# Sums of weight quarters by accumulating DMAs in a one-level Strassen-Winograd MLP product

## The chip, the cores and the metric

The kernel runs on one core of a Trainium2 chip. The metric is the device time of one execution in microseconds (us). Its engines have queues of their own: TensorE (PE; its weight loads are listed as PEld), VectorE (DVE), ScalarE (ACT), GpSimd (POOL) and SyncE (SP), which here only issues DMAs.

## What is computed

One layer of a decoder trunk for 512 tokens of width 1024, all in float32: a norm, an input projection, a pooling mixer and a sparse attention mixer that are merged by gates, and an MLP. The change touches the first product of the MLP:

```
h = rms_norm(x, norm_mlp[l])
x = x + jnp.square(jax.nn.relu(h @ w_ff1[l])) @ w_ff2[l]
return rms_norm(x, norm_final)
```

`w_ff1` is 1024 x 4096 and `w_ff2` 4096 x 1024.

## The kernel before

Every float32 matrix is used as a high part (rounded to float32r by ScalarE's copy) and a low part (the rest, a subtraction on VectorE), and every product is three matmuls: high x high, high x low, low x high.

**The stages.** Input projection, attention and mixers come first. Then the output projection `wo` is applied (`tm3` and `tm3_resident`, line 1226), the residual is normed and turned by `to_fm` (lines 1189 to 1217), and four chunks of the MLP follow, c = 0 to 3 (lines 1320 to 1376). A chunk makes 1024 hidden columns in two groups of 512 (the first MLP product), and then multiplies them by 1024 rows of `w_ff2` (the second, keys `f2...`, eight weight blocks).

**A group.** A group is the product of a 1024 x 512 piece of `w_ff1` with the turned activations, done as one level of Strassen-Winograd with seven products in place of eight. The piece is cut into four quarters of 512 x 256: "21" is columns half 2, rows half 1, and so on. Seven weight operands are made: A11, A12, A22 are quarters, and S1 = 21 + 22, S2 = S1 - 11, S3 = 11 - 21, S4 = 12 - S2. The activations have T1 to T4 likewise (`XB`, `XT`, lines 1211 to 1216), each split into high and low once. `product` (1235) runs 24 matmuls on 256 tokens for one operand. The class `Group` (1248) combines the results: `s` is a copy of the A11 result, `u2 = S2 result + s`, `u3 = S3 result + u2`, and so on; `NEEDS` says that A22 comes after `u3` and S4 after the last sum. `act` (1307) takes relu, square and the split of the result.

**The order of products.** Chunk 0 uses `FIRST` (line 136): A11 and A12 of both groups, then S1, S3, S2 of each group, then A22, S4 of each, since T1 to T4 are finished late there. Chunks 1 to 3 run group 0 and then group 1 in the order `IN_TURN` (line 137): A11, S2, S3, S1, A12, A22, S4.

**Loading and preparing weights.** `LD` is the list of loads in order and `WL` the list of weight operands in order of use. A load (`emit_load`, 167) goes to the SP queue into one of eight 512 KB buffers: four called `raw` and, in this part of the kernel, four pieces of `oT`. When an operand has been made from a buffer, `give_back` (197) lends it to the next load. `group_steps` (216) prepares an operand of a group: ScalarE's copy to the high part (line 226), VectorE's subtraction for the low part (228), and, in four places, the sums of quarters on VectorE: line 231 makes S1 in a spare piece of `GB`, 233 makes S3, 235 makes S2, 238 makes S4. Prepared operands lie in three slots (`w`, twice, and `w3`). `ahead` (294) is called between matmuls and prepares at most the two operands behind the one in use, since a slot is free only when the product three places back is done. Other weight blocks are prepared in halves by `emit_prep_half` (lines 277 and 279; in the earlier stage the second half's low part is on GpSimd).

**What sets the order on the engines.** The program gives an order of instructions, with generators in `side` stepped between matmuls (`step_side`). A scheduler then places each instruction in its engine's queue by its own estimate of when its inputs are ready, so an instruction can stand earlier or later than written. Each queue runs in order, and an instruction that waits holds up those behind it.

Of the kernel before, what the change touches and what calls it, by code (L numbers as in the profile page):

```python
# [62 lines left out]
def trunk(ctx: ExitStack, tc: tile.TileContext, A, out):  # L63
# [70 lines left out]
            add_rows(f"wo{h}{i}", w_o, 256 * i, 512 * h)  # L134
    GROUPS = {}
    FIRST = ("A11", "A12"), ("S1", "S3", "S2"), ("A22", "S4")
    IN_TURN = ("A11", "S2", "S3", "S1", "A12", "A22", "S4")

    def add_group(c, g):

        c0 = 1024 * c + 512 * g
        GROUPS[c, g] = {"raw": {}, "at": {}}
        for q in ("11", "21", "22", "12"):
            r0, o = 512 * (int(q[1]) - 1), c0 + 256 * (int(q[0]) - 1)
            GROUPS[c, g]["at"][q] = len(LD)
            LD.append(([(w_f1[r0:r0 + 512, o:o + 256].rearrange("(k p) c -> p k c", p=128), 0)], (c, g, q)))

    for c in range(4):
        for g in range(2):
# [42 lines left out]

    def strassen_on():

        return st["load"] >= GROUPS[0, 0]["at"]["11"]

    def give_back(*tiles):
        spare.extend(tiles)
# [6 lines left out]
    def slot_of(i):  # L205
# [7 lines left out]
            return slots_hl[-1]  # L213
        return [wp.tile([128, 1024], FR, tag=f"w{e}", bufs=2, name=f"w{e}{i}") for e in "hl"]

    def group_steps(i):

        c, g, o = WL[i][1]
        G = GROUPS[c, g]
        while len(G["raw"]) < 4:  # L220
            assert emit_load()
        r = G["raw"]
        sm = GBf[:, 1024 + 1024 * g:2048 + 1024 * g]
        src = {"A11": r["11"], "A12": r["12"], "A22": r["22"], "S1": sm, "S2": r["11"], "S3": r["21"], "S4": r["12"]}[o]
        h, l = slot_of(i)
        ACT.activation(h, src, AF.Copy)
        yield
        DVE.tensor_tensor(l, src, h.bitcast(F32), op=ALU.subtract)
        if o == "A11":
            yield  # L230
            DVE.tensor_tensor(sm, r["21"], r["22"], op=ALU.add)
            yield
            DVE.tensor_tensor(r["21"], r["11"], r["21"], op=ALU.subtract)
            yield
            DVE.tensor_tensor(r["11"], sm, r["11"], op=ALU.subtract)
        elif o == "A12":
            yield
            DVE.tensor_tensor(r["12"], r["12"], r["11"], op=ALU.subtract)
        G["done"] = G.get("done", "") + o
        dead = {"S3": "21", "A22": "22", "S4": "12"}.get(o)  # L240
        if o in ("A12", "S2") and "A12" in G["done"] and "S2" in G["done"]:
            dead = "11"
        hls[i] = tuple(x.rearrange("p (a b) -> p a b", a=4) for x in (h, l))
        if dead:
            give_back(r[dead])

    def emit_prep_half():

        i = st["prep"]
        if i >= len(WL):  # L250
            return
        if not isinstance(WL[i][1], int):
            if "gen" not in part:
                part["gen"] = group_steps(i)
            if next(part["gen"], True):
                part.clear()
                st["prep"] += 1
            return
        at = WL[i][1]
        if "h" not in part:  # L260
            while st["load"] <= at:
                assert emit_load()
            if WL[i][0] in dest:
                h, l = dest[WL[i][0]][:2]
            else:
                h, l = slot_of(i)
            part.update(h=h, l=l, half=0)
        h, l = part["h"], part["l"]
        t, a, b = raws[at]
        n = a * b  # L270
        cut = (a // 2) * b
        sl = slice(0, cut) if part["half"] == 0 else slice(cut, n)
        if sl.stop > sl.start:
            if mode["first"]:
                POOL.tensor_scalar(h[:, sl], t[:, sl], 1.0, 1.0, op0=ALU.mult, op1=ALU.mult)
            else:
                ACT.activation(h[:, sl], t[:, sl], AF.Copy)  # L277
            eng = POOL if mode["first"] or part["half"] and mode["pool"] else DVE
            eng.tensor_tensor(l[:, sl], t[:, sl], h[:, sl].bitcast(F32), op=ALU.subtract)  # L279
        if part["half"] == 0:  # L280
            part["half"] = 1
            return
        part.clear()
        st["prep"] += 1
        raws.pop(at)
        if st["load"] > RAW + GROUPS[0, 0]["at"]["11"]:
            give_back(t)
        else:
            emit_load()
            if st["kept"] == RAW:  # L290
                give_back()
        hls[i] = (h[:, :n].rearrange("p (a b) -> p a b", a=a), l[:, :n].rearrange("p (a b) -> p a b", a=a))
# [873 lines left out]
    with ExitStack() as c3:  # L1166
        q3 = c3.enter_context(pool("q3"))
        mT = (q3.tile([128, 8, S], FR, name="mH"), q3.tile([128, 8, S], FR, name="mL"))
        W1 = (q3.tile([128, 8, S], FR, name="W1H"), q3.tile([128, 8, S], FR, name="W1L"))
        keep([f"wo1{i}" for i in range(4)], W1)  # L1170
        ACT.activation(tick, GB[:, 7, 0:1], AF.Sqrt)

        def split_m(j):
            ACT.activation(mT[0][:, j, :], GB[:, j, :], AF.Copy)
            DVE.tensor_tensor(mT[1][:, j, :], GB[:, j, :], mT[0][:, j, :].bitcast(F32), op=ALU.subtract)
        split_m(0)
        split_m(1)
        for j in range(2, 8):
            def post(ps, j=j):
                merge(j, ps)  # L1180
                split_m(j)
            fm3(f"pn{j}", post, OT)

        def post0(t, ps):
            add_x(t, 0, ps)
            square_sum(t, 0)
        tm3("wo", 0, mT, post0)

        def to_fm(t):
            xs = q3.tile([128, D], F32, tag="xs", bufs=1, name="xs")  # L1190
            add_x(t, 1, PS1[t])
            square_sum(t, 1)
            normed(t, xs)
            for _ in range(5):
                yield
            th, sl = t // 2, slice(128 * (t % 2), 128 * (t % 2) + 128)
            for a in range(2):
                pt = bank()
                for k in range(4):
                    PE.transpose(pt[:, 128 * k:128 * k + 128], xs[:, 512 * a + 128 * k:512 * a + 128 * k + 128], ident)  # L1200
                src = pt[:, :].rearrange("p (k c) -> p k c", k=4)
                b = f"{a + 1}{th + 1}"
                if b != "12":
                    ACT.activation(XB[b][0][:, :, sl], src, AF.Copy)
                ACT.activation(XQ[b][:, :, sl], src, AF.Copy)
                if b != "12":
                    DVE.tensor_tensor(XB[b][1][:, :, sl], src, XB[b][0][:, :, sl].bitcast(F32), op=ALU.subtract)
                yield
            if th == 0:
                return  # L1210
            for o, d, x, y in (("T1", XT, XQ["12"], XQ["11"]), ("T3", XQ["12"], XQ["22"], XQ["12"]),
                               ("T2", XQ["11"], XQ["22"], XT), ("T4", XQ["21"], XQ["21"], XQ["11"])):
                DVE.tensor_tensor(d[:, :, sl], x[:, :, sl], y[:, :, sl], op=ALU.subtract)
                ACT.activation(XB[o][0][:, :, sl], d[:, :, sl], AF.Copy)  # L1214
                yield
                DVE.tensor_tensor(XB[o][1][:, :, sl], d[:, :, sl], XB[o][0][:, :, sl].bitcast(F32), op=ALU.subtract)
            turned[0] += t == 3

        PS1 = {}

        def post1(t, ps):
            PS1[t] = ps
            g = to_fm(t)
            next(g)
            side.append(g)
        tm3_resident("wo", 1, mT, post1)
# [21 lines left out]
    class Group:  # L1248


        def __init__(self, c, g, aT):
            self.c, self.g, self.aT = c, g, aT
            self.s = pair(GBf, 6 + g)
            self.u2, self.u3, self.c21 = pair(MAf, 6 + g), pair(MAf, g), pair(MAf, 2 + g)
            self.ps, self.done = {}, set()
# [21 lines left out]
        def main(self):  # L1277
# [4 lines left out]
            while "S2" not in self.done:  # L1282
                yield
            yield
            DVE.tensor_tensor(self.u2, self.ps["b"], self.s, op=ALU.add)
            while "S3" not in self.done:
                yield
            yield
# [18 lines left out]
        def act(self, src, f, th):  # L1307
            yield
            r = p4.tile([128, 512], F32, tag="r", bufs=2, name="r")
            ACT.activation(r, src, AF.Relu)  # L1310
            ACT.activation(r, r, AF.Square)
            hi, lo = (x[:, 4 * self.g + 2 * f:4 * self.g + 2 * f + 2, 256 * th:256 * th + 256] for x in self.aT)
            r = r.rearrange("p (f t) -> p f t", f=2)
            ACT.activation(hi, r, AF.Copy)
            yield
            yield
            DVE.tensor_tensor(lo, r, hi.bitcast(F32), op=ALU.subtract)
# [77 lines left out]
```

## Time and profile before

| | |
|---|---|
| median of 3 runs | 828.61 us (827.01 to 829.36) |
| the profiled execution | 829.27 us, its span 827.5 us |
| PE busy | 801.9 us (97%) |
| DVE, ACT, POOL busy | 569.8, 459.8, 166.2 us |
| mean granted clock of TensorE | 0.994 |
| read from HBM | 72.81 MB, 91 GB/s over the span |

A row of the order of time (timeline) gives the start in us, the duration in us, the engine, the line, the operation, the tiles (output <- inputs), shapes and a count of merged instructions, and in brackets how long the engine was idle before it and what ended that. A row of a table by line ends with busy time and mean ns of one, then the idle time before it with what released it. A row of waits reads "who waited, for whom: us in total, times, longest". A row of DMA issues ends with KB each and the median us from issue to landing. Busy time of matmuls is modelled, and their bars overlap.

### The profile page before, as it was taken

The numbers are of one execution on the slowest core, as the hardware profiler recorded it, in microseconds if no ns is written. First come the engines' busy times: TensorE is split into PE (matmuls) and PEld (weight loads), VectorE is DVE, ScalarE is ACT, GpSimd is POOL, SyncE is SP. The second block draws the span as 40 slices with busy tenths as digits, with TensorE's granted clock in tenths as the row PEclk, the third lists the DMA queues.
The fourth block names the chain that finished last, engine by engine and source line by source line (L and its number), as shares of the span: only waits on it lengthen the run. The fifth ranks groups of instructions, "written<-read, shape, count | busy, mean of one in ns | idle before, by whom it ended". The sixth has DMA issues, their size and how long they took to land.

```text
span 827.5 us, 12810 instructions
## 1 busy us (share of the span) xinstructions
PE 801.9 (97%) x4649; PEld 695.0 (84%) x4649; DVE 569.8 (69%) x1155; ACT 459.8 (56%) x945; POOL 166.2 (20%) x235
## 2 busy tenths in 40 slices
PE   7999999999998999999999989999999999999997
PEld 4889878887887888888787879889988899889986
DVE  7797744537978888887674788646864586458813
ACT  6566443337868888898333584622761376227711
POOL 6000000027765756652223000000000000000000
PEclk9999999999999999999999999999999999999999
DMA  9363632331030101115425004431353035313202
GB/s 304 96 178 114 183 90 89 103 96 44 14 90 27 40 26 40 47 58 178 153 77 178 1 26 162 147 99 30 116 161 100 28 102 159 97 51 103 78 0 103
DMA packets 83289, 78.36 MB, mean 95 GB/s; under 512 B 3573, under 2 KB 69657, under 8 KB 83226
## 3 DMA queue, kind: packets, MB, share of 16 engines
q1 hardware_dynamic: 82938, 76.75, 30.2%
q8 instruction: 37, 0.61, 0.3%
q10 hardware_dynamic: 288, 0.79, 0.3%
q14 instruction: 26, 0.21, 0.1%
HBM read 72.81 MB, written 2.10 MB: 91 GB/s over the span
## 4 chain that ended last, share of the span: by engine, by line
PE 80%; DVE 8%; ACT 4%; POOL 2%; issue 2%; DMA 2%; SPq 0%; POOLq 0%; ACTq 0%; DVEq 0%
PE psB L320 27%; PE psF L320 20%; PE psB L1241 18%; PE psO L1003 3%; PE psT L969 3%; PE psS L908 2%; PE psV L320 2%; DVE P L930 2%; DVE PT L984 1%; DMA raw<-w_out 1%; PE psF L374 1%; PE psC L608 1%; POOL P L953 1%; DVE x L457 1%; POOL wl L279 1%
## 5 line engine op out<-in xcount | busy, mean ns | idle before, releaser
L320 PE MATMUL psF<-R,wh 128*128 128x512 f32 x512 | 166.3, 404 | 0.2 <-ACT MA L766 0.2
L277 ACT ACTIVATE wh<-raw 128x512 fp32r<-128x512 f32 (+1 forms) x116 | 70.1, 620 | 101.8 <-PE psF L320 35.6
L320 PEld LDWEIGHTS psF<-R,wh 128*128 128x128 f32 x512 | 92.4, 189 | 17.8 <-ACT MA L766 0.5
L320 PE MATMUL psF<-R,wl 128*128 128x512 f32 x256 | 102.0, 398 | 0.8 <-DVE wl L279 0.8
L279 DVE TENSOR_TENSOR wl<-raw,wh 128x512 fp32r<-128x512 f32 (+1 forms) x92 | 65.4, 721 | 51.4 <-ACT wh L277 51.0
L953 POOL TENSOR_SCALAR P<-P,sm,GT 128x128 f32<-128x128 f32 (+3 forms) x128 | 83.1, 657 | 56.6 <-DVE sm L950 39.3
L320 PE MATMUL psB<-wh,aT 128*128 128x512 f32 x288 | 92.1, 395 | 0.0
L940 ACT ACTIVATE P<-P,sm 128x128 f32<-128x128 f32 (+3 forms) x128 | 71.1, 558 | 14.7 <-DVE sm L930 14.0
L1363 POOL TENSOR_TENSOR MA<-x,gB 128x512 f32<-128x512 f32 x1 | 1.3, 1287 | 350.7 <-DVE sq L1156 350.7
L1241 PE MATMUL psB<-R,wh 128*128 128x256 f32 x352 | 65.4, 286 | 2.3 <-ACT R L1214 2.1
L320 PEld LDWEIGHTS psB<-wh,aT 128*128 128x128 f32 x288 | 54.1, 188 | 12.8
L930 DVE CUSTOM_DVE_ANT_0 P<-psS,cst 128x128 f32<-128x128 f32 (+3 forms) x128 | 59.7, 484 | 5.2 <-PE psT L969 3.8
L279 POOL TENSOR_TENSOR wl<-raw,wh 128x512 fp32r<-128x512 f32 x28 | 38.7, 1387 | 106.0 <-ACT wh L277 103.6
L984 DVE TENSOR_TENSOR PT<-psT,PT 128x512 fp32r<-128x512 f32 (+2 forms) x96 | 56.6, 594 | 4.5 <-ACT PT L980 3.4
L320 PEld LDWEIGHTS psF<-R,wl 128*128 128x128 f32 x256 | 48.3, 189 | 11.8 <-DVE wl L279 0.9
L1241 PEld LDWEIGHTS psB<-R,wh 128*128 128x128 f32 x352 | 55.4, 192 | 3.0 <-ACT R L1214 2.3
L320 PE MATMUL psB<-wl,aT 128*128 128x512 f32 x144 | 56.9, 395 | 0.0
L980 ACT ACTIVATE PT<-psT 128x512 fp32r<-128x512 f32 (+2 forms) x96 | 49.2, 520 | 11.7 <-PE psT L969 10.9
L969 PE MATMUL psT<-ident,P 128*128 128x128 f32 x320 | 51.3, 275 | 3.4 <-POOL P L953 3.0
L969 PEld LDWEIGHTS psT<-ident,P 128*128 128x128 f32 x320 | 39.8, 141 | 13.8 <-POOL P L953 5.4
L320 PE MATMUL psB<-w3h,aT 128*128 128x512 f32 x160 | 51.0, 390 | 0.0
L1241 PE MATMUL psB<-R,wl 128*128 128x256 f32 x176 | 50.0, 284 | 0.0
(293 smaller groups left out, 1957.2 us busy)
## 6 DMA issues: line engine op xcount, KB each, us to landing
raw<-w_in SPq DMA_DIRECT2D x32, 512.0 KB, 3.8
oT<-w_ff SPq DMA_DIRECT2D x32, 512.0 KB, 3.9
raw<-w_ff SPq DMA_DIRECT2D x32, 512.0 KB, 3.6
raw<-w_proj_nsa SPq DMA_DIRECT2D x8, 512.0 KB, 3.8
raw<-w_out SPq DMA_DIRECT2D x8, 512.0 KB, 3.6
x<-x SPq DMA_DIRECT2D x7, 512.0 KB, 6.7
rs<-rx SPq DMA_DIRECT2D x40, 64.0 KB, 2.0
raw<-w_ck SPq DMA_DIRECT2D x4, 512.0 KB, 7.1
```

Of the source, the lines that this page charges most:

```text
L277: ACT.activation(h[:, sl], t[:, sl], AF.Copy)
L279: eng.tensor_tensor(l[:, sl], t[:, sl], h[:, sl].bitcast(F32), op=ALU.subtract)
L320: PE.matmul(ps, a, b, start=first and j == 0, stop=last and j == n - 1, skip_group_check=True)
L908: PE.matmul(ps[:, 0:n], q, rhs, start=a, stop=not a, skip_group_check=True)
L930: DVE.tensor_tensor_reduce(out=P[:, o:o + n].rearrange("p (a c) -> p a c", c=128), in0=s, in1=m, scale=1.0, scalar=3e38, op0=ALU.add, op1= ...
L940: last_exp[:] = [ACT.activation(c, c, AF.Exp, bias=sm[:, 0, e:e + 1], scale=-1.0, accum_out=sm[:, 1, e:e + 1])]
L953: POOL.tensor_scalar(P[:, o:o + n], P[:, o:o + n], sm[:, 2, e:e + 1], GT[:, qb, c + e:c + e + 1], op0=ALU.mult, op1=ALU.mult)
L969: PE.transpose(pt[:, 128 * j:128 * j + 128], P[:, 128 * j:128 * j + 128], ident)
L980: ACT.activation(dH, src, AF.Copy)
L984: DVE.tensor_tensor(dL, src, dH.bitcast(F32), op=ALU.subtract)
L1003: PE.matmul(ps[:, qb % 2, :, :], VV[:, k, b, g, :], t[:, j, :, :], start=False, stop=last and j == len(kbs) - 1 and t is tL, skip_group_ch ...
L1241: PE.matmul(ps[:, 256 * f:256 * f + 256], w[u][:, k, 128 * f:128 * f + 128], XB[x][v][:, k, :], start=first and n == 0, stop=n == 23, skip ...
```

## The change

The four sums of a group are no longer made by VectorE. Instead GpSimd's queue issues DMAs that read a quarter from HBM again and add it to a quarter that already lies in a buffer (`accum_op=ALU.add`). Such a DMA can only add, so the columns of half 2 are taken with the opposite sign: S1 = 21 + 22 as before, S3 = 11 + 21, S2 = S1 + 11, S4 = S2 + 12. T1 and T4 are turned in sign, T2 is an addition, `u2` is `s` minus the S2 result, and the results of half 2 come out negated, which `act` undoes with a scale of -1 in its relu.

The sums are made in place: S1 in the buffer of quarter 21; S3 in that of 11 after A11 has been prepared; S2 in S1's after S1 has been prepared; S4 in S2's after S2 has been prepared. So each of these three stands between two preparations. The first sum of a group is issued ahead by `first_sum`: for group 1 of a chunk after A22 of group 0 is prepared, for group 0 of the next chunk when the seventh of the eight `f2` blocks is prepared, and otherwise at the group's first step. The order in chunks 1 to 3 becomes A11, S1, S3, S2, A12, A22, S4, and the quarters are loaded in the order 21, 11, 12, 22.

```diff
-    IN_TURN = ("A11", "S2", "S3", "S1", "A12", "A22", "S4")
+    IN_TURN = ("A11", "S1", "S3", "S2", "A12", "A22", "S4")
...
-        for q in ("11", "21", "22", "12"):
+        for q in ("21", "11", "12", "22"):
...
+    def add_onto(c, g, to, q):
+
+        G = GROUPS[c, g]
+        POOL.dma_start(G["raw"][to].rearrange("p (k c) -> p k c", k=4), G["of"][q], accum_op=ALU.add)
+
+    def first_sum(c, g):
+        if (c, g) in GROUPS and "21" in GROUPS[c, g]["raw"] and not GROUPS[c, g]["summed"]:
+            GROUPS[c, g]["summed"] = "S1"
+            add_onto(c, g, "21", "22")
...
-        sm = GBf[:, 1024 + 1024 * g:2048 + 1024 * g]
-        src = {"A11": r["11"], "A12": r["12"], "A22": r["22"], "S1": sm, "S2": r["11"], "S3": r["21"], "S4": r["12"]}[o]
+        first_sum(c, g)
+        q = {"A11": "11", "S3": "11", "A12": "12", "A22": "22"}.get(o, "21")
+        src = r[q]
         h, l = slot_of(i)
         ACT.activation(h, src, AF.Copy)
         yield
         DVE.tensor_tensor(l, src, h.bitcast(F32), op=ALU.subtract)
-        if o == "A11":
-            yield
-            DVE.tensor_tensor(sm, r["21"], r["22"], op=ALU.add)
-            yield
-            DVE.tensor_tensor(r["21"], r["11"], r["21"], op=ALU.subtract)
-            yield
-            DVE.tensor_tensor(r["11"], sm, r["11"], op=ALU.subtract)
-        elif o == "A12":
-            yield
-            DVE.tensor_tensor(r["12"], r["12"], r["11"], op=ALU.subtract)
...
+        more = {"A11": ("11", "21"), "S1": ("21", "11"), "S2": ("21", "12")}.get(o)
+        if more:
+            yield
+            add_onto(c, g, *more)
+        else:
+            give_back(src)
+        if o == "A22":
+            first_sum(c + g, 1 - g)
...
+        if WL[i][0][:2] == "f2" and WL[i][0][3:] == "12":
+            first_sum(int(WL[i][0][2]) + 1, 0)
...
-            for o, d, x, y in (("T1", XT, XQ["12"], XQ["11"]), ("T3", XQ["12"], XQ["22"], XQ["12"]),
-                               ("T2", XQ["11"], XQ["22"], XT), ("T4", XQ["21"], XQ["21"], XQ["11"])):
-                DVE.tensor_tensor(d[:, :, sl], x[:, :, sl], y[:, :, sl], op=ALU.subtract)
+            for o, d, x, y in (("T1", XT, XQ["11"], XQ["12"]), ("T3", XQ["12"], XQ["22"], XQ["12"]),
+                               ("T2", XQ["11"], XQ["22"], XT), ("T4", XQ["21"], XQ["11"], XQ["21"])):
+                DVE.tensor_tensor(d[:, :, sl], x[:, :, sl], y[:, :, sl], op=ALU.add if o == "T2" else ALU.subtract)
...
-            DVE.tensor_tensor(self.u2, self.ps["b"], self.s, op=ALU.add)
+            DVE.tensor_tensor(self.u2, self.s, self.ps["b"], op=ALU.subtract)
...
-            ACT.activation(r, src, AF.Relu)
+            ACT.activation(r, src, AF.Relu, scale=-1.0 if f else 1.0)
```

More of the change, by code (lines that the diff above doesn't have):

```diff
@@ L136, in trunk @@
     FIRST = ("A11", "A12"), ("S1", "S3", "S2"), ("A22", "S4")
-    IN_TURN = ("A11", "S2", "S3", "S1", "A12", "A22", "S4")
+    IN_TURN = ("A11", "S1", "S3", "S2", "A12", "A22", "S4")
     def add_group(c, g):
         c0 = 1024 * c + 512 * g
-        GROUPS[c, g] = {"raw": {}, "at": {}}
-        for q in ("11", "21", "22", "12"):
+        GROUPS[c, g] = {"raw": {}, "at": {}, "of": {}, "summed": ""}
+        for q in ("21", "11", "12", "22"):
             r0, o = 512 * (int(q[1]) - 1), c0 + 256 * (int(q[0]) - 1)
             GROUPS[c, g]["at"][q] = len(LD)
-            LD.append(([(w_f1[r0:r0 + 512, o:o + 256].rearrange("(k p) c -> p k c", p=128), 0)], (c, g, q)))
+            GROUPS[c, g]["of"][q] = w_f1[r0:r0 + 512, o:o + 256].rearrange("(k p) c -> p k c", p=128)
+            LD.append(([(GROUPS[c, g]["of"][q], 0)], (c, g, q)))
     for c in range(4):
@@ L193, in strassen_on @@
     def strassen_on():
-        return st["load"] >= GROUPS[0, 0]["at"]["11"]
+        return st["load"] >= GROUPS[0, 0]["at"]["21"]
     def give_back(*tiles):
@@ L228, in group_steps @@
         DVE.tensor_tensor(l, src, h.bitcast(F32), op=ALU.subtract)
-        if o == "A11":
+        hls[i] = tuple(x.rearrange("p (a b) -> p a b", a=4) for x in (h, l))
+        more = {"A11": ("11", "21"), "S1": ("21", "11"), "S2": ("21", "12")}.get(o)
+        if more:
             yield
-            DVE.tensor_tensor(sm, r["21"], r["22"], op=ALU.add)
-            yield
-            DVE.tensor_tensor(r["21"], r["11"], r["21"], op=ALU.subtract)
-            yield
-            DVE.tensor_tensor(r["11"], sm, r["11"], op=ALU.subtract)
-        elif o == "A12":
-            yield
[L238 to L245, printed above, removed]
+            add_onto(c, g, *more)
[3 more added lines that the diff above has]
+            first_sum(c + g, 1 - g)
     def emit_prep_half():
@@ L285, in emit_prep_half @@
         raws.pop(at)
-        if st["load"] > RAW + GROUPS[0, 0]["at"]["11"]:
+        if WL[i][0][:2] == "f2" and WL[i][0][3:] == "12":
+            first_sum(int(WL[i][0][2]) + 1, 0)
+        if st["load"] > RAW + GROUPS[0, 0]["at"]["21"]:
             give_back(t)
```

## The prediction

> **What bounds the kernel now.** I read the page first (busy shares), then the table of windows from 500 us on, then the waits of PE, and last the order of time of each engine.
>
> ```profile
> span 827.5 us, 12810 instructions
> PE 801.9 (97%) x4649; PEld 695.0 (84%) x4649; DVE 569.8 (69%) x1155; ACT 459.8 (56%) x945; POOL 166.2 (20%) x235
> 500.00:530.00 30.00, 30.00 (x230) 28.93 (x229) 22.99 (x30) 20.47 (x32) 0.00 (x0) 1.00 0.55 182
> ...
> sum 290.00, PE 290.00 PEld 262.63 DVE 189.66 ACT 140.31 POOL 0.00; mean PE 58.00 PEld 52.53 DVE 37.93 ACT 28.06 POOL 0.00
> ```
>
> TensorE is busy 97% of the span. In the windows the columns are PE, PEld, DVE, ACT, POOL, granted clock, DMA share, GB/s. From 500 to 790 us, nearly all of the MLP, PE has 290.00 of 290.00 us at clock 1.00: no time that VectorE saves there can shorten the run. The GpSimd queue is empty, so there is room for the issues that are added. What PE loses around the MLP's start it loses between 480 and 500 us:
>
> ```profile
> 480.00:490.00 10.00, 8.65 (x74) 8.44 (x73) 10.00 (x14) 8.42 (x14) 0.00 (x0) 1.00 0.17 54
> 490.00:500.00 10.00, 7.74 (x52) 7.25 (x51) 9.80 (x15) 7.45 (x12) 0.00 (x0) 0.83 0.10 33
> PE psB L1241 <- ACT R L1214: 2.1, 1, 2.1
> PE psB L1241 <- DVE w3l L228: 1.4, 1, 1.4
> 493.36 0.53 PE L1241 MATMUL psB<-R,wh 128*128 128x256 f32 x1 [2.06 <-ACT R L1214]
> 494.69 0.63 PE L1241 MATMUL psB<-R,wh 128*128 128x256 f32 x2
> ...
> 496.61 0.52 PE L1241 MATMUL psB<-R,wh 128*128 128x256 f32 x2
> ```
>
> There VectorE is full (10.00 and 9.80 of 10). PE waits 1.4 us for the low half of A12's weights and 2.06 us (then 0.2 for L1216) for T1, the first product's activations. After that the clock is 0.83 in the window: a pair of matmuls takes 0.63 us at 494.69 where a pair takes 0.40 elsewhere (658.20 to 661.06 below gives 0.12 a matmul). From 493.36 to 496.61 there are some 15 matmuls in 3.25 us, 1.8 at the usual pace, so about 1.5 us lost. The whole T1 wait costs 2.06 + 0.2 + 1.5, some 3.7 us.
>
> **The change, part by part.** Removed: four sums on VectorE in each of eight groups, 32 in all.
>
> ```profile
> L231 DVE TENSOR_TENSOR GB<-raw,oT 128x1024 f32<-128x1024 f32 x6 | 7.4, 1226 | 17.8 <-DMA oT<-w_ff 17.8
> L235 DVE TENSOR_TENSOR raw<-GB,raw 128x1024 f32<-128x1024 f32 x6 | 7.4, 1226 | 0.2
> L238 DVE TENSOR_TENSOR oT<-oT,raw 128x1024 f32<-128x1024 f32 x6 | 7.3, 1224 | 0.2
> L233 DVE TENSOR_TENSOR raw<-raw,raw 128x1024 f32<-128x1024 f32 x6 | 7.3, 1219 | 0.0
> ```
>
> These are the 24 of chunks 1 to 3, 29.4 us; with the first chunk's eight, 32 x 1.22 = 39 us of VectorE. By the windows 24 of them are worth **nothing**: PE has no idle time there. Of the other eight two, both L238, stand in the full stretch; the other six are over by 461.5 us, and VectorE pauses soon after:
>
> ```profile
> 460.24 1.23 DVE L235 TENSOR_TENSOR oT<-GB,oT 128x1024 f32<-128x1024 f32 x1
> 463.24 0.16 DVE L1161 RECIPROCAL sq<-sq 128x1 f32<-128x1 f32 x1 [1.18 <-ACT sq L1160]
> ...
> 486.04 1.22 DVE L238 TENSOR_TENSOR raw<-raw,raw 128x1024 f32<-128x1024 f32 x1
> ...
> 488.98 1.22 DVE L238 TENSOR_TENSOR oT<-oT 128x1024 f32<-128x1024 f32 x1
> 490.11 0.69 DVE L1216 TENSOR_TENSOR xT4L<-MA,xT4H 128x512 fp32r<-128x512 f32 x1
> 490.71 0.69 DVE L1213 TENSOR_TENSOR GB<-MA 128x512 f32<-128x512 f32 x1
> 491.31 1.23 DVE L228 TENSOR_TENSOR wl<-GB,wh 128x1024 fp32r<-128x1024 f32 x1
> 491.02 0.28 PE L1241 MATMUL psB<-R,wl 128*128 128x256 f32 x1
> ```
>
> The L1213 at 490.71 makes the last half of T1. Without the two sums it, and S1's low half behind it, come 2.4 us earlier, T1 is split by about 491.1, when A12 of group 1 ends on PE (the last row), and the 3.7 us go. The 1.4 us wait stays: none of the sums lies ahead of it in that stretch. Turned signs (L1213, L1285, the -1 in L1310) are the same instructions with another operation: nothing. **Gain 3.7 us.**
>
> Added: 32 accumulating DMAs of 512 KB from GpSimd's queue, 16.8 MB more to read. The DMA share from 500 to 530 us is 0.55 (windows above), and the last 428 us move 39.46 MB at 92 GB/s (first row below), so the rate alone is no limit. What counts is how long one takes, for each stands between two weight preparations: S3 is summed into A11's own buffer once A11's low half is made from it, S2 into S1's, S4 into S2's. I call L the time from the end of that low half to the sum landed. The trace has no DMA from this queue and no accumulating one. The nearest rows:
>
> ```profile
> DMA packets 27602, 39.46 MB, mean 92 GB/s; under 512 B 1216, under 2 KB 16565, under 8 KB 27573
> raw<-w_ff SPq DMA_DIRECT2D x32, 512.0 KB, 3.6
> rs<-rx SPq DMA_DIRECT2D x40, 64.0 KB, 2.0
> x<-x SPq DMA_DIRECT2D x7, 512.0 KB, 6.7
> L279 POOL TENSOR_TENSOR wl<-raw,wh 128x512 fp32r<-128x512 f32 x28 | 38.7, 1387 | 106.0 <-ACT wh L277 103.6
> ```
>
> 64 KB take 2.0 us and 512 KB 3.6, so 512 KB are 1.83 us of moving (1.6 x 512/448) and 1.77 fixed. An accumulating DMA reads both its source and its destination: moving estimated at twice that, 3.66. GpSimd has to write out 512 runs of 1 KB (128 partitions x 4); GpSimd's rows give 1.4 us for a pass over 512 columns; one pass, or two because the reading side has two streams: 1.4 to 2.8, I take 2.1. **L = 1.77 + 3.66 + 2.1, about 7.5 us**, an estimate. Low end 3.6 (a plain load, the issue free); high end 13: the crowded loads' 6.7 with its moving part doubled, 1.77 + 9.9, and an issue of 1.4.
>
> By the Trainium skill (DMA: Bandwidth & Descriptors, Anatomy of one DMA) a DMA from GpSimd takes 2.0 us and its bytes at 436 GB/s, 3.2 us for 512 KB; Collectives: The Full Stack (The bandwidth ceiling) says that an adding DMA halves the rate because it reads two sources. An estimate from both is 2.0 + 2.4 = 4.4 us, below every limit worked out next; the rows here have no such DMA to set against it.
>
> What L may be without a stall:
>
> ```profile
> 655.37 0.28 PE L1241 MATMUL psB<-xT2H,wh 128*128 128x256 f32 x1
> 658.20 0.29 PE L1241 MATMUL psB<-xT3H,wh 128*128 128x256 f32 x1
> 661.06 0.40 PE L1241 MATMUL psB<-R,w3h 128*128 128x256 f32 x2
> 672.49 0.40 PE L1241 MATMUL psB<-R,wh 128*128 128x256 f32 x2
> 642.60 1.23 DVE L228 TENSOR_TENSOR w3l<-raw,w3h 128x1024 fp32r<-128x1024 f32 x1 [2.98 <-ACT w3h L226]
> 648.24 1.23 DVE L228 TENSOR_TENSOR wl<-raw,wh 128x1024 fp32r<-128x1024 f32 x1 [3.15 <-ACT wh L226]
> 666.88 1.04 ACT L226 ACTIVATE wh<-raw 128x1024 fp32r<-128x1024 f32 x1
> 667.96 1.23 DVE L228 TENSOR_TENSOR wl<-raw,wh 128x1024 fp32r<-128x1024 f32 x1 [0.26 <-ACT wh L226]
> ```
>
> One product is 2.86 us (658.20 to 661.06). A preparation is 2.31 us from 666.88 to 669.19, and its product's third matmul, 0.24 us in, needs the low half. Group 1 of this chunk starts at 672.49. Its S3, third in the new order, starts 5.72 later, at 678.2; its buffer must have landed by 678.2 + 0.24 - 2.31 = 676.1. A11's low half ended at 669.19: **L may be 6.9**. S2 comes one product later and hangs on S1, one product later: the same, some 6.8. Group 0 of a chunk has more: its A11 is prepared while the blocks of the second MLP product still run: its low half ends at 643.83 and its S3 starts at 658.2: 12.3. S2 starts at 661.06 there and hangs on the chunk's second preparation, which ends at 649.47: 9.5. S4 of each group some 9.3 (three products after S2). The first sum, of 21 and 22, waits only for a load and has over 10 us. The new order asks that VectorE makes u2 and u3 (0.69 each) between S2 and A22: one product lies between, 2.86 against 1.4.
>
> So at L = 7.5 group 1 of chunks 1 to 3 stalls 0.6 to 0.7 us at S3, which moves the limit of S2 too, and 0.1 there: **0.8 x 3 = 2.4 us**. What waits is ACT's high-half copy, and behind it in ACT's queue the squares of the group before; these have no early consumer.
>
> The first chunk is tighter, since its S1 is late. S1's low half ends at 492.5 - 2.4 = 490.1; S2's sum lands at 497.6, its low half at 499.9. PE, free of the T1 wait, runs S1 from 491.1 and S3 from 494.0, and wants S2's at 497.1: **2.8 us**. In group 1 the copy of S1 stands behind S2's on ACT (done 499.8), its low half behind S2's on DVE (done 501.1): S2's sum lands at 508.6, is prepared at 510.9, wanted at 508.4: **2.5 us**. I count neither at a lower clock: each splits into a wait for the high and one for the low half, like the 1.4 us wait that kept 1.00.
>
> Sum: -3.7 + 2.4 + 2.8 + 2.5 = **+4.0 us**. The profiled execution took 829.27 us (span 827.5 and 1.8 around it), so 833.3; it lies 0.7 above the median 828.61, so 832.6 on that. I say 833.
>
> **The rivals.** (1) *The sums land in time.* The point from which it decides: L below about 4.7 in the first chunk (497.1 - 2.31 - 490.1) and 6.8 later. Then only the 3.7 us of T1 are left to count: 829.27 - 3.7 = 825.6; with L at 6, the first chunk gives 2.3 back (1.3 and 1.0): 827.9. For it: a plain load's 3.6 us; against: two streams and an issue in software. This is the side where the run is not slower. The two pages named above, with 4.4 us, speak for it. (2) *L near 10.* Chunks 1 to 3: 3.1 at S3 of group 1 and 0.5 at S2 of group 0, 3.6 x 3 = 10.8; first chunk 5.3 + 5.0 - 3.7 = 6.6; the five stalls over 2 us also cost the clock, 1.5 each: 7.5. Sum 24.9: 854. At L = 9 without the clock's loss: 2.1 x 3 + 4.6 = 10.9, so 840. For it: nothing in the trace caps L, and the loads of a crowded moment took 6.7. (3) *GpSimd's issue gets in front of its own splitting.* At 446.62 a low half on GpSimd is next in the chain:
>
> ```profile
> 446.62 1.30 POOL wl L279
> ...
> 447.97 17.20 PE psB L320 x74
> ```
>
> If the first sum of group 0, whose load lands about then, is placed ahead of it, PE waits for as long as the issue takes, 1.4 to 2.8 us, on top of one of the others: with the forecast, 835. (4) *The order of the products absorbs it.* The scheduler already mixes products:
>
> ```profile
> 498.15 0.28 PE L1241 MATMUL psB<-xT3H,w3h 128*128 128x256 f32 x1
> ...
> 498.38 0.27 PE L1241 MATMUL psB<-xT2H,wh 128*128 128x256 f32 x1
> ```
>
> Here S2's matmuls stand among S3's. So A22 of group 0 could stand before S2 of group 1. Then the 2.5 us go and the run is 830.8, no change.
>
> **Chances.** Forecast, L 6.5 to 8.5, with or without (3): 0.42 (829 to 838). Rival 1: 0.25 (824.5 to 828). Rival 2: 0.25 (838 to 862), of which 0.06 above 856. Rival 4: 0.08 (829 to 831). About 0.3%, 2.5 us, is what a measurement can tell from no change. Faster by more: most of rival 1, 0.22. Within: its rest, rival 4 and the low edge of the forecast, 0.18. Slower: 0.60. The range for 8 in 10 is 824.5 to 856.
>
> **What would show it.** The DMA issues: 32 from POOL's queue with their time to landing; under 6 us refutes the middle of my sum, over 9 makes rival 2. The waits of PE: the 2.06 us on L1214 gone; new ones of L1241 on ACT's high halves at S3 and S2 of each second group, 0.5 to 1 us, larger in the first chunk. ACT's waits at L226 for a DMA. PE at 290 of 290 from 500 on would prove rival 1. Chunk 1 to 3 must be equal among themselves. I am wrong if a sum is issued late for the queue's order, not for its own length.

## The result, and the profile after

The changed kernel takes 858.87 us (median of 4 runs, 856.72 to 864.18) against 828.99 for the kernel before: a ratio of 1.037, 95% interval 1.032 to 1.043. It is **slower by 3.7%**; 833 was forecast. The profiled execution took 864.18 us, the slowest of the four, with a span of 862.4, 34.9 us more than before. So single microseconds of it should not be pressed.

The page of the changed kernel, the lines that answer to those of before:

```profile
span 862.4 us, 12862 instructions
PE 814.0 (94%) x4649; PEld 703.8 (82%) x4649; DVE 535.7 (62%) x1123; ACT 458.0 (53%) x945; POOL 207.8 (24%) x267
...
q0 software_dynamic: 16896, 16.78, 12.8%
...
L220 POOL DMA_DIRECT2D raw<-w_ff x18 | 23.1, 1285 | 181.2 <-DVE w3l L241 40.3
...
raw<-w_ff POOLq DMA_DIRECT2D x18, 512.0 KB, 6.8
oT<-w_ff POOLq DMA_DIRECT2D x14, 512.0 KB, 5.8
```

VectorE lost 32 instructions and 34 us of busy time as meant, and the span grew. q0 is the DMA queue that GpSimd feeds (packets, MB, share of the 16 DMA engines). The 32 new DMAs are the last two rows: 6.8 and 5.8 us in the median from issue to landing. GpSimd is busy 1.28 us with each.

The table of windows and the waits of PE of the changed kernel:

```profile
500.00:790.00 290.00, 274.55 (x1706) 247.95 (x1705) 144.50 (x183) 121.86 (x180) 34.16 (x27) 0.97 0.61 140
```

```profile
PE psB L1248 <- DVE MA L1302: 15.1, 4, 5.3
PE psB L327 <- POOL wl L284: 3.7, 2, 3.5
PE psB L1248 <- DVE wl L241: 2.8, 5, 0.8
PE psB L1248 <- ACT wh L239: 2.4, 2, 2.1
PE psB L1248 <- DVE w3l L241: 1.9, 2, 1.4
```

PE is no longer full between 500 and 790 us, and its clock is 0.97 there. The 2.1 us wait on L1214 is gone, but one new wait is larger than all else: four times up to 5.3 us on L1302, the last of the additions ahead of S4 (S1's result onto `u3`). In the changed kernel L239 and L241 are an operand's high and low half, L284 the low half of other blocks, L220 the accumulating DMA, L187 a load from SP, L1248 a product.

**Where the 34.9 us lie.** The order of time of PE shows where each run of first-product matmuls begins and ends. A prime marks an operand of a chunk's second group. For all the kernels of this study (profiled executions, us; the second product takes 44.5 to 45.2 a chunk in the five profiles read for it, before and after among them):

| kernel | time | span | MLP begins | chunk 0 | 1 | 2 | 3 |
|---|---|---|---|---|---|---|---|
| before | 829.27 | 827.5 | 476.4 | 47.6 | 40.1 | 40.1 | 40.1 |
| after | 864.18 | 862.4 | 482.5 | 48.7 | 49.1 | 47.7 | 50.3 |
| no sums | 824.90 | 823.1 | 474.7 | 44.8 | 40.1 | 40.1 | 40.1 |
| no S4 sums | 837.90 | 836.1 | 480.7 | 48.8 | 41.7 | 40.7 | 40.9 |
| S4 sums only | 825.66 | 823.9 | 475.4 | 44.9 | 40.1 | 40.1 | 40.1 |
| plain copies | 834.37 | 832.6 | 481.6 | 45.4 | 40.1 | 40.1 | 41.7 |
| hold without effect | 859.73 | 857.9 | 482.7 | 47.1 | 48.4 | 48.1 | 47.7 |
| loads held | 842.91 | 841.1 | 482.2 | 47.2 | 43.5 | 42.1 | 42.4 |
| u3 first | 850.06 | 848.3 | 480.9 | 48.5 | 46.5 | 45.8 | 42.5 |
| first sum late | 852.65 | 850.8 | 475.7 | 47.4 | 48.9 | 48.1 | 46.9 |
| late and held | 835.22 | 833.4 | 475.4 | 47.2 | 42.6 | 42.2 | 42.3 |
| all three | 831.48 | 829.7 | 477.6 | 47.1 | 40.9 | 40.1 | 40.3 |
| before, S4 of chunk 0 by DMA | 826.89 | 825.1 | 476.7 | 44.8 | 40.1 | 40.1 | 40.1 |
| before, S4 of chunk 0 later | 828.10 | 826.3 | 478.0 | 44.8 | 40.1 | 40.1 | 40.1 |

After against before: the MLP begins 6.1 us later, chunk 0 is 1.2 longer, chunks 1 to 3 are 8.9, 7.6 and 10.2 longer, and what follows chunk 3's first product is 0.8 longer: 34.8 of the 34.9.

**One stall, read row by row.** Chunk 2, group 1, in the order of time of the changed kernel:

```profile
698.64 1.28 POOL L220 DMA_DIRECT2D raw<-w_ff  x1 [7.58 <-DVE wl L241]
...
699.36 0.37 SPq L187 DMA_DIRECT2D oT<-w_ff  x1
...
706.54 0.28 PE L1248 MATMUL psB<-xT4H,w3l 128*128 128x256 f32 x1
...
708.36 1.06 ACT L239 ACTIVATE wh<-raw 128x1024 fp32r<-128x1024 f32 x1 [9.53 <-DMA raw<-w_ff]
...
709.45 1.23 DVE L241 TENSOR_TENSOR wl<-raw,wh 128x1024 fp32r<-128x1024 f32 x1 [6.88 <-ACT wh L239]
...
710.59 0.68 DVE L1302 TENSOR_TENSOR MA<-psB,MA 128x512 f32<-128x512 f32 x1
...
711.42 0.77 PE L1248 MATMUL psB<-R,wh 128*128 128x256 f32 x2 [4.60 <-DVE MA L1302]
```

GpSimd issues the sum for S4' at 698.64, 0.44 us after S2's low half. PE's last matmul of A22' starts at 706.54, and PE needs S4' next. The sum lands at about 708.3; only then do the high half (708.36) and the low half (709.45) follow. L1302 has to read S1's result out of PSUM, the memory for PE's results, before PE may add S4's to it there (both use `ps["d"]`); VectorE's queue has it behind S4's low half, so it comes at 710.59 and PE starts at 711.42. The row of PE names L1302, but the chain behind it is the DMA.

This DMA took 9.6 us. The DMA view of the same stretch (698 to 709 us) shows what ran beside it:

```profile
q1 hardware_dynamic: 544, 1.05, 32.8%
q0 software_dynamic: 528, 0.52, 30.2%
...
raw<-w_ff POOLq DMA_DIRECT2D x1, 512.0 KB, 9.6
oT<-w_ff SPq DMA_DIRECT2D x1, 512.0 KB
raw<-w_ff SPq DMA_DIRECT2D x1, 512.0 KB, 8.3
```

SP's queue (q1) moves 1.05 MB meanwhile: two plain loads, issued at 699.36 and 700.49 because A12' and A22' had just freed their buffers. In the packet records the sum's first packet comes 3.96 us after its issue, against 2.0 when nothing is beside it, and its last after 9.27. The load suffers as well: 8.3 us.

Then the clock (windows of the changed kernel):

```profile
707.00:710.00 3.00, 0.00 (x0) 0.00 (x0) 0.55 (x1) 1.64 (x3) 0.00 (x0) 0.85 0.17 53
710.00:713.00 3.00, 1.58 (x7) 1.61 (x8) 3.00 (x5) 2.15 (x5) 0.00 (x0) 0.50 0.32 101
713.00:716.00 3.00, 3.00 (x16) 3.00 (x15) 2.06 (x5) 3.00 (x7) 0.00 (x0) 0.51 0.73 230
716.00:719.00 3.00, 3.00 (x17) 2.52 (x16) 2.96 (x5) 2.97 (x7) 1.28 (x1) 1.00 0.47 140
```

PE works again from 711.42, at half clock until about 716. The chunk's first product is 7.6 us longer in all: the stall of 4.6, a wait of 0.54 for S2's low half ahead of it, and some 2.5 behind it, most of them the clock. The three low windows add up to 6.8 us at half clock (0.15, 0.50 and 0.49 of 3 us, doubled). By the Trainium skill (TensorE: Matmul & The Clock Gate, Part 1) the clock halves after an idle window of about 3.4 us. These rows agree with the half; but 2.13 us of idle before 506.66 in this same profile were followed by 0.62 and 0.81 in the windows 507 to 510 and 510 to 513, 3.4 us at half clock, so here less than 3.4 was enough. The length of the idle time does not settle it either: 2.20 us before 499.97 in the kernel called "first sum late" kept 1.00, and 1.74 us before 504.73 in "u3 first" were followed by 3.4 us at half clock.

**The start.** The order of time of the changed kernel around 450 us, GpSimd's queue:

```profile
441.85 3.00 POOL L284 TENSOR_TENSOR W1L<-raw,W1H 128x512 fp32r<-128x512 f32 x2
...
449.29 1.31 POOL L220 DMA_DIRECT2D raw<-w_ff  x1 [4.45 <-DMA raw<-w_ff]
450.13 1.79 POOL L284 TENSOR_TENSOR wl<-raw,wh 128x512 fp32r<-128x512 f32 x1
...
451.97 0.79 PE L327 MATMUL psB<-wl,mH 128*128 128x512 f32 x1 [3.51 <-POOL wl L284]
```

The first sum of chunk 0 stands in GpSimd's queue ahead of a low half that PE wants. It waits 4.45 us at the head of the queue for the load of the quarter it adds to. PE stands 3.51 us, and the clock is 0.83 over 440 to 460.

### The profile page after: what moved, and what is told of

Read it like the earlier page. It is cut to its first block, busy times and chain, and to the rows that moved or that the text cites. A ratio compares the mean times of both kernels' runs of the same rounds, so it can differ in the third digit from the quotient of the medians.

```text
span 862.4 us, 12862 instructions
## 1 busy us (share of the span) xinstructions
PE 814.0 (94%) x4649; PEld 703.8 (82%) x4649; DVE 535.7 (62%) x1123; ACT 458.0 (53%) x945; POOL 207.8 (24%) x267
## 5 line engine op out<-in xcount | busy, mean ns | idle before, releaser
L282 ACT ACTIVATE wh<-raw 128x512 fp32r<-128x512 f32 (+1 forms) x120 | 72.5, 622 | 107.3 <-PE psF L327 35.6
L284 DVE TENSOR_TENSOR wl<-raw,wh 128x512 fp32r<-128x512 f32 (+1 forms) x96 | 68.5, 725 | 56.9 <-ACT wh L282 56.6
L1248 PE MATMUL psB<-R,wh 128*128 128x256 f32 x352 | 68.3, 295 | 9.7 <-DVE MA L1302 9.7
L220 POOL DMA_DIRECT2D raw<-w_ff x18 | 23.1, 1285 | 181.2 <-DVE w3l L241 40.3
L1248 PEld LDWEIGHTS psB<-R,wh 128*128 128x128 f32 x352 | 57.8, 201 | 10.5 <-ACT wh L282 4.8
L284 POOL TENSOR_TENSOR wl<-raw,wh 128x512 fp32r<-128x512 f32 x28 | 38.9, 1393 | 104.0 <-ACT wh L282 104.0
L1248 PE MATMUL psB<-R,wl 128*128 128x256 f32 x176 | 51.5, 293 | 0.8 <-DVE wl L241 0.8
```

Source lines behind the costliest of these rows:

```text
L220: POOL.dma_start(G["raw"][to].rearrange("p (k c) -> p k c", k=4), G["of"][q], accum_op=ALU.add)
L1248: PE.matmul(ps[:, 256 * f:256 * f + 256], w[u][:, k, 128 * f:128 * f + 128], XB[x][v][:, k, :], start=first and n == 0, stop=n == 23, skip ...
```

## The experiments

**Which sums cost.** All 32 out, only S4's eight out, only S4's eight kept. They read each quarter as it is in place of the sum.

```diff
 # no sums: first line of add_onto
+        return
 # no S4 sums
+        if q == "12":
+            return
 # S4 sums only
+        if q != "12":
+            return
```

> The changed kernel with all 32 accumulating DMAs left out, so that S1 to S4 are unsummed quarters; the new order of products, the turned signs and the loads stay. Theory A (the sums arrive late, S4's most of all) and theory B (every sum on the path costs its own time): the whole loss goes, span 823 to 826, that is the 3.7 us of T1 gained against 827.5. Theory D (the new order of products, or the new order of loads, costs time by itself): above 835.

> The changed kernel with only S4's sum left out (8 of 32), S4 being made from S2's buffer as it is. Theory A: what chunks 1 to 3 lose is S4's sum in the second group, which lands 10.4 us after its issue; they lose 2 us or less each in place of 8.9, 7.6 and 10.2, the 6.1 us before the MLP stay, span about 838. Theory B (S3's and S2's sums are the stall and S4's only shows it): chunks keep half of the loss or more, span 850.

> The changed kernel with S4's sum alone (8 of 32); S1, S2, S3 are made from buffers without their sums. Theory A in its full form (S4 is late because S2 was prepared late behind the two sums before it, and slow beside plain loads; neither alone is enough): S2 is prepared on time, S4's sum has some 9.3 us, stalls of 1 us or less a chunk, span 826 to 831. If the slow transfer beside loads is enough by itself: 3 to 4 us and the clock in each chunk, span 840 to 845.

Measured: 824.90, 837.90 and 825.66 us, beside 830.01 for before on the same chip. The waits of PE from 400 us on without the S4 sums:

```profile
PE psB L329 <- POOL wl L286: 3.2, 1, 3.2
PE psB L1250 <- DVE wl L243: 2.2, 4, 0.7
PE psB L1250 <- ACT wh L241: 2.1, 1, 2.1
PE psB L1250 <- DVE w3l L243: 1.9, 2, 1.4
```

and with the S4 sums only:

```profile
PE psB L1250 <- DVE w3l L243: 1.4, 1, 1.4
PE psB L1250 <- DVE wl L243: 0.8, 1, 0.8
```

Without the sums the changed kernel is faster than before (one run each): the gain on VectorE is there. The S4 sums alone are nearly free, and chunks 1 to 3 take 40.1. Without them the long waits are gone and chunks 1 to 3 lose 1.6, 0.6 and 0.8 us, while the start and chunk 0 keep their loss. So the 27 us of chunks 1 to 3 belong to **neither alone**. The S3 and S2 sums make S2's operand late, which leaves S4's sum little time; by itself that sum has room. It also lands sooner. With the S4 sums only, chunk 2's S4' goes out 25.8 us after the chunk's first matmul in place of 29.9, and SP's next two loads come 2.3 and 5.2 us behind it in place of 0.7 and 1.9:

```profile
raw<-w_ff POOLq DMA_DIRECT2D x1, 512.0 KB, 6.2
```

So the lateness of S2 does two things: it shortens S4's time, and it bunches the preparations of A12' and A22' so that their buffers' next loads run beside the sum. In chunks 1 to 3 each kind of sum costs little without the other.

**The loads beside S4's sum.** The buffers of A12' and A22' are to be given back only behind S4'.

```diff
+        elif c and g and o in ("A12", "A22"):
+            held.append(src)
         else:
             give_back(src)
+            if o == "S4":
+                give_back(*held)
+                held.clear()
```

> The changed kernel, but in the second group of chunks 1 to 3 the buffers of A12 and A22 are lent to the next loads only after S4 is prepared, so that no plain load runs beside S4's sum. Theory A: S4's sum lands in 6 to 6.5 us in place of 9.4 to 10.4, the stall at S4 falls from 5.3, 4.6 and 3.6 to 1 to 2 us and the slow clock after it goes: 5 us a chunk, span 845 to 849. If the sum's time does not come from the loads: no change, 860. If the held loads come late for the second product: a wait of PE on L282 or L284 in it.

Measured 859.73 us. This run **missed**: written later in the program, the loads were still placed early by the scheduler, since nothing tied them to S4. They went out at 697.33 and 698.46, beside S4's sum (696.61), which took over 10 us again. It tells nothing of the theory. The second form ties them: a small write by VectorE into each buffer, queued behind S4's low half, has to come before the load.

```diff
+            if o == "S4" and held:
+                with tc.issue_after(low.ins):
+                    for t in held:
+                        DVE.memset(t[:, 0:8], 0.0)
+                give_back(*held)
+                held.clear()
```

> The loads into A12's and A22's buffers of the second group in chunks 1 to 3 are now truly held: a tiny write to each buffer is queued on VectorE behind S4's low half, and the loads wait for it (in the run before, they were issued as soon as the buffers were free, next to the sum as ever). Theory A: without plain loads beside it S4's sum lands in 6 to 6.5 us in place of about 10; S4 stalls 1 to 2 us, the clock is not lost; chunks lose 1.5 to 2.5 us each in place of 7.6 to 10.2, span 840 to 846. If S2's lateness alone is the cause: sum at 6 but the stall still 4 us and more. If the sum's time does not come from the loads: no change, span 858 to 862.

Measured 842.91 us. The same place in its order of time, and the DMA view from 690 to 698.5 us:

```profile
691.22 1.28 POOL L220 DMA_DIRECT2D raw<-w_ff  x1 [7.52 <-DVE wl L243]
...
697.37 1.06 ACT L241 ACTIVATE wh<-raw 128x1024 fp32r<-128x1024 f32 x1 [5.95 <-DMA raw<-w_ff]
...
698.47 1.23 DVE L243 TENSOR_TENSOR wl<-raw,wh 128x1024 fp32r<-128x1024 f32 x1 [3.31 <-ACT wh L241]
...
699.64 0.68 DVE L1312 TENSOR_TENSOR MA<-psB,MA 128x512 f32<-128x512 f32 x1
...
700.47 0.47 PE L1258 MATMUL psB<-R,wh 128*128 128x256 f32 x2 [1.06 <-DVE MA L1312]
```

```profile
q0 software_dynamic: 528, 0.52, 41.2%
...
raw<-w_ff POOLq DMA_DIRECT2D x1, 512.0 KB, 6.0
```

Nothing of SP's queue runs beside the sum; it takes 6.0 us in place of 9.6, the stall is 1.06 in place of 4.60, and the clock stays at 1.00 (window 698 to 701). Chunks 1 to 3 fall from 147.1 to 128.1 us. With S2 as late as it is, the loads beside the sum cost 19 us. The Trainium skill (DMA: Bandwidth & Descriptors, Queues, rings and completion order) says that a DMA engine takes turns between queues packet by packet; that both transfers are slowed fits it. That the first packet can come 2 us later is not explained by it, and no run here separates why.

**S4's low half behind the last addition.** L1302, which completes `u3`, is queued in front of S4's low half ("u3 first" in the table).

```diff
+        if o == "S4":
+            while (c, g) not in last_u:
+                yield
+            with tc.issue_after(last_u[c, g]):
+                DVE.tensor_tensor(l, src, h.bitcast(F32), op=ALU.subtract)
...
```

(`last_u` is set at that addition.)

> The changed kernel, with the low half of S4 queued on VectorE behind the addition that S4's product needs (L1302 in the changed kernel), not ahead of it. Theory C (PE waits 15.1 us for L1302 because it stands behind S4's low half): most of the loss in chunks 1 to 3 goes, span 840 to 845. Theory A (S4's own weights are as late as that): PE then waits for S4's high half in place of L1302, about 1 us less each time, span 857 to 860.

Measured 850.06 us, between what the two theories gave. The waits of PE:

```profile
PE psB L1256 <- ACT wh L241: 5.1, 3, 2.2
...
PE psB L1256 <- ACT w3h L241: 3.1, 1, 3.1
```

The wait on L1302 is gone, and PE waits for S4's high half instead: the sum still lands late, 10.2 and 9.6 us after issue in chunks 1 and 2 with some 540 packets of SP's loads beside it. So the order on VectorE adds to each stall, and the landing makes it.

**The start.** The first sum of chunk 0 is queued behind GpSimd's last low half.

```diff
+            if (c, g) == (0, 0):
+                with tc.issue_after(last_pool[0]):
+                    add_onto(c, g, "21", "22")
...
```

(`last_pool` holds GpSimd's latest low half.)

> The changed kernel; one DMA is moved: the first sum of group 0 of chunk 0 is queued on GpSimd behind the last low half that GpSimd makes for the output projection. Theory: the 6.1 us before the MLP are this DMA waiting at the head of GpSimd's queue for its load, with PE's weights behind it; they go, the MLP starts at 476 to 477 in place of 482.5, span 855 to 857. If they come from the DMA's traffic or the order of loads: the start stays near 482. The sum itself then lands later, but S1 of chunk 0 is needed only 40 us on.

Measured 852.65 us; the MLP begins at 475.7, 1.0 us behind the kernel without any sum. Its GpSimd queue:

```profile
445.95 1.30 POOL L289 TENSOR_TENSOR wl<-raw,wh 128x512 fp32r<-128x512 f32 x1 [2.55 <-issue]
447.21 1.29 POOL L289 TENSOR_TENSOR W1L<-raw,W1H 128x512 fp32r<-128x512 f32 x1
...
448.44 1.29 POOL L221 DMA_DIRECT2D raw<-w_ff  x1
```

The sum is issued at 448.44 and waits for nothing. The MLP begins 6.8 us earlier than in the changed kernel, but not all of that is the place of the sum: the same matmul 200 places before the MLP's first starts at 431.33 in the changed kernel and at 430.17 here, ahead of anything that the edit moves. The wrong place cost the other 5.6 us: 3.5 of waiting, and about 2 for the clock, which was at half from 449.7 to 456.5 there, 4.6 us of it with PE at work; here it is 1.00 over 440 to 460.

**Adding or moving.** The same 32 DMAs as plain copies (S1 to S4 are then not formed).

```diff
-        POOL.dma_start(G["raw"][to]..., G["of"][q], accum_op=ALU.add)
+        POOL.dma_start(G["raw"][to]..., G["of"][q])
```

> The changed kernel with the 32 DMAs as plain copies from the same queue, that is the quarter is written over the buffer and not added. It prices the adding: issue 1.28 us and first packet at 2.0 us as before; the 512 packets should take about half of the adding DMA's 3.5 us. Landing at 4.3 to 4.8 us in place of 6.2; then S3 and S2 are in time, S4 follows on time, chunks lose under 1.5 us each, the 6.1 at the start stay: span 830 to 835. If the software queue itself is the slow part: landing over 5.5 us and span over 845.

Measured 834.37 us. Its page:

```profile
q0 software_dynamic: 4608, 16.78, 6.3%
...
L220 POOL DMA_DIRECT2D raw<-w_ff x18 | 13.5, 752 | 175.1 <-DVE w3l L241 39.6
...
raw<-w_ff POOLq DMA_DIRECT2D x18, 512.0 KB, 4.2
```

A plain copy from the same queue lands in 4.2 us, is issued in 0.75 and has 144 packets; adding makes that 5.5 to 6.4 with nothing beside it, 1.28 and 528. With 4.2 us all copies of chunks 1 to 3 are in time but one (chunk 3 41.7): S4' of chunk 3, which had a load issued 0.2 us behind it and landed after 7.0. The start keeps its loss, for it is a matter of place and not of length.

**Do the causes add?** The late first sum and the held loads together; then also u3 first.

> All 32 accumulating DMAs, the first sum of chunk 0 queued behind GpSimd's last low half, and the loads freed by A12 and A22 of each second group held until S4's low half is made. If the start and the loads beside S4's sum are separate causes, their effects add by stage: the start as in the run with the late first sum (475.7), chunk 0 about 47.3, chunks 1 to 3 as in the run with the held loads (43.5, 42.1, 42.4): span 834.6, time about 836.4. If one of them hid the other, the span stays above 840.

> As the run before it in this list, and S4's low half queued behind the third addition on VectorE. If the 1.1 to 1.3 us that S4 still waited with held loads came from that addition standing behind S4's low half, chunks 1 to 3 fall by about 1.2 each: span near 831, time near 833. The rival: the waits move to ScalarE's high halves, as they did when only this reordering was made, and the time stays at 836 or above. Either way the time should not come below 825, that of the version without any of the DMAs.

Measured: 839.16 us (2 runs, 835.22 and 843.11; ratio 1.012, interval 1.000 to 1.023), and **831.86** (8 runs, 829.34 to 834.12; ratio 1.0025, 1.0005 to 1.0044), so still a little slower than before. The first is at its forecast by stages, span 833.4 for 834.6 expected, though its second run lay 8 us higher. The second fell by 3.7 us of span where 3.6 were expected, but that match is luck: chunks 1 to 3 fell by 5.8, and the MLP began 2.2 later (477.6 for 475.4), which the edit does not touch: PE was about as much later at the matmul 200 places ahead (432.02 for 429.70). Its waits of PE from 400 us on:

```profile
PE psB L1272 <- ACT wh L247: 1.9, 1, 1.9
PE psB L1272 <- DVE w3l L255: 1.4, 1, 1.4
PE psB L1272 <- DVE wl L255: 1.1, 2, 0.8
```

With all 32 sums in place, chunks 1 to 3 take 40.9, 40.1 and 40.3. In chunk 2 the sum for S2' was issued 20.0 us after the chunk's first matmul in place of 21.0, and S4's 28.8 in place of 29.9. So the reordering gained in two ways, by the addition and by this 1 us, which were not taken apart.

**What is worth keeping.** Only the pair of sums that delayed T1 needs to move. Either chunk 0's two S4 sums become DMAs (signs as in the change; all other sums stay on VectorE), or they stay on VectorE, without any DMA, and are queued behind S2's low half.

```diff
 # by DMA
+        elif o == "S2" and not c:
+            yield
+            POOL.dma_start(r["11"]..., G["of12"], accum_op=ALU.add)
 # later
-        elif o == "A12":
+        elif o == "A12" and c or o == "S2" and not c:
             yield
-            DVE.tensor_tensor(r["12"], r["12"], r["11"], op=ALU.subtract)
+            with tc.issue_after(low.ins):
+                DVE.tensor_tensor(r["12"], r["12"], r["11"], op=ALU.subtract)
```

> The kernel before with the turned signs, and with two accumulating DMAs in all: S4 of the two groups of chunk 0 (into S2's buffer once S2 is prepared); the other 30 sums stay on VectorE, in the order of before. It takes only the two L238 out of VectorE's full stretch at 480 to 500 us. Theory (the gain of the change is these two alone, 3.7 us with the clock): 823.5 to 826 against 828.6, a ratio of 0.995 to 0.997. If the gain of the kernels without or with few DMAs came from the removal of the other sums: no change, 827.5 to 829.

> The kernel before with its own signs and no accumulating DMA: the two sums for S4 of chunk 0 stay on VectorE but are queued behind S2's low half, after the full stretch. The same theory: the gain is a matter of place and not of the DMA, 824 to 826.5. If VectorE is short of time right after as well: PE waits in S2 or S3 of group 1 for low halves, 827 to 829.

Measured 826.95 us (10 runs) and 826.59 (9 runs), against 829.38 for before (18 runs): ratios 0.9968, intervals 0.9956 to 0.9979 and 0.9953 to 0.9983. Both beat both kernels, by 2.4 to 2.8 us. The waits of PE from 400 us on in the second:

```profile
PE psB L1242 <- DVE w3l L228: 1.4, 1, 1.4
PE psB L1242 <- DVE wl L228: 0.8, 1, 0.8
```

The 1.4 us for A12 stays, the wait for T1 is replaced by one of 0.8 that does not touch the clock, and chunk 0 takes 44.8 in place of 47.6. The whole useful part of the change needs no DMA.

## Why the prediction was wrong, step by step

- **The gain, 3.7 us.** Right in place, a little large. The wait for T1 and its clock loss go; chunk 0 gets 2.7 us shorter (47.6 to 44.8), since a wait of 0.8 for S1's low half is next in line. The 2.4 us of the version with two DMAs agree.
- **L = 7.5 us.** Too long for a DMA alone: 0.44 from low half to issue and 5.5 to 6.4 to landing give 5.9 to 6.8 (S4's with held loads 0.4 + 6.0). Moving was sized well: 3.66 forecast, 3.2 to 4.1 from the first packet to the end of the last with nothing beside it (528 packets of about 0.105 us on 16 engines are 3.5). The issue and the fixed part were too large: 2.1 + 1.77 forecast, against 0.44, 2.0 from the start of the issue to the first packet, its 1.28 included, and 0.3 behind the last packet. The estimate of 4.4 from the two pages of the Trainium skill was too low; a plain copy from this queue took 4.2, where the first of them (DMA: Bandwidth & Descriptors, Anatomy of one DMA) gives 3.2.
- **S3 and S2 in chunks 1 to 3, 0.8 each.** Right in size: 1.6, 0.6 and 0.8 without the S4 sums.
- **Chunk 0, 2.8 + 2.5.** 3.9 was measured (48.8 without the S4 sums against 44.9 with them alone), in one wait of 2.1 for a high half, small ones, and in the changed kernel a clock of 0.62 and 0.81 in the two windows behind it (507 to 513 us). I had counted no clock there, and my rival 2 had put the bound at 2 us. No such bound shows: five other kernels of the table wait 1.9 to 2.2 us at this place and keep 1.00, and their chunk 0 takes 47.1 to 47.4.
- **S4, "some 9.3".** **This step failed**, with it the forecast. The limit was worked out as if S2 were prepared a whole product ahead: three products of 2.86 less a preparation of 2.31 are only 6.3 when S2's low half ends just as PE wants it. The text itself let the sums of S3 and S2 come just in time; then S2's low half ends late, A12' and A22' are prepared at once behind it, and S4's limit is about 6.4: the last matmul of A22' starts at 706.54, S4' could follow 0.12 later, its low half 0.24 after that, a preparation is 2.31, and S2's low half ended at 698.20. I put one L into each limit separately and did not carry a delay on to the next link of the chain S1, S2, S4.
- **L as one number.** The second half of the same failure. With S2 late, A12' and A22' free two buffers just when S4's sum is issued; the loads that follow stretch it from 6.0 to 9.6. Rival 2's "loads of a crowded moment" has the right mechanism with a wrong place: it made S3, not S4, late. Its 854 came near for the wrong reasons: S3 never waited 3.1 us in chunks 1 to 3, and at its L of 10 it left out what S4 would have waited beyond its own 9.3.
- **A stall's second price.** The four waits on L1302 are 5.3, 4.6, 3.6 and 1.5 us, 15.1 in all; with the 3.0 of S3 and S2 that is 18 of the 26.7 us that chunks 1 to 3 lost. Of the other 8.7 the clock explains most: it was at half for 6.8 us around the end of each of the three long ones, and PE worked 4.3, 4.5 and 6.0 us of that. At the pace of 508 to 511 us (0.21 us a matmul in place of 0.12) this loses about 6.5 in all, an estimate; some 2 stay open. I had counted none.
- **Rival 3, the start.** Right in place; its price was 5.6, not 1.4 to 2.8. I priced the issue alone, which took 1.3. What cost was that an instruction that waits for a load blocks its queue: 4.45 us, and the clock.
- **Rival 4.** Not seen. Chunks 1 to 3 were to be equal among themselves; with loads in the way they are not (49.1, 47.7, 50.3).
- **"Issued late for the queue's order"** was named as what would prove me wrong. At the start it did; S4's sums were issued promptly and landed late.

Left open: why the first packet comes later beside SP's loads, when a wait of about 2 us costs clock and when not, and which part of the last reordering gained the last 5.8 us of chunks 1 to 3.

## What to carry to other kernels

A transfer put between two links of a chain has to be checked against the limit that is left when the link before it runs late, and with whatever its neighbours free at that moment: sums that cost 3 us or nothing alone became a 27 us loss together. A DMA that must wait for a load is placed behind the queue's other work, and a buffer's next load can be tied to a later instruction when an urgent transfer is under way. Before moving work off an engine, look for the one instance that delays something: here two of 32 sums held all the gain, and moving those two down in the same queue got it.

## What the hardware showed

- An accumulating DMA of 512 KB into SBUF: 528 packets, 1.28 us of GpSimd, first packet 2.0 us after the issue begins, landed in 5.5 to 6.4 us when alone; the same as a plain copy: 144 packets, 0.75, 1.46, 4.2.
- Two plain loads issued within about 2 us behind it: 9.6 to 10.7 us for the sum, and 8.3 for the load in the stall shown; the sum's first packet came 2.0 to 4.3 us after issue in such cases.
- The granted clock: 6.8 us at half around the end of 4.60 us of idle PE, 3.4 us at half behind 2.13 and behind 1.74, unchanged after 1.06, 1.88 and 2.20. In these runs the length of the idle time alone does not tell which.
